# A copy kernel with staged batches: six buffers for four, loads and stores in long runs, remainders eight batches late

## The chip, the cores and the metric

The kernel runs on one core of a Trainium2 chip. The metric is the device time of one execution in microseconds (us); lower is better. A *span* is the length of one profiled execution; it is about 1.8 us shorter than the time of the same run. For the kernel before, its span of 757.3 us would go with some 759 us (an estimate from that 1.8), 2 us above its median: the first profile before is one of its slower executions.

## The reference, cut to what matters

```python
batch, length, dim = (32, 4096, 256)          # float32
window_size, stride = 64, 32
n_windows = (length - window_size) // stride + 1      # 127
for i in range(n_windows):
    start = i * stride
    result[:, i] = x[:, start:start + window_size].copy()
```

It is pure copying. A batch of x is 128 blocks of 32 rows, 32 KB each; a window is two neighbouring blocks, 64 KB. So almost every block is written twice.

## The kernel before: the parts that matter

There are two ways for a batch, on two queues.

- **Direct** (21 batches, issued from the Sync engine, q1 in the profile): DRAM to DRAM copies of 16 windows at a time, seven of them a batch. Some are split in two copies, of the first and the second halves of the windows. Fifteen windows remain: the *remainder*.
- **Staged** (11 batches, issued from the Scalar engine, q10 in the profile): the batch is loaded once into a buffer of 128 partitions and stored twice, once for the first halves of the windows, once for the second halves.

A staged store writes 128 half windows where only 127 are its own. The odd one spills into the neighbouring batch, so a remainder of that neighbour may be written only after the stores have landed. That is why the remainders are late, and why they wait.

```python
class Staging:
    ...
    def load(self, q, g):
        n, i = divmod(g, len(self.tiles))
        if n:
            q.wait_ge(self.stored[i], 32 * n)
        self.c.load(q, self.tiles[i], self.batches[g]).then_inc(self.loaded[i], 16)

    def store(self, q, g):
        n, i = divmod(g, len(self.tiles))
        q.wait_ge(self.loaded[i], 16 * (n + 1))
        ...  # the last batch: four smaller stores
        for half in (0, 1):
            self.c.store(q, self.tiles[i], self.batches[g], half).then_inc(self.stored[i], 16)

    def run(self, q):
        bufs = len(self.tiles)
        for g in range(min(bufs, len(self.batches))):
            self.load(q, g)
        for g in range(len(self.batches)):
            self.store(q, g)

            if g >= 1 and g - 1 + bufs < len(self.batches):
                self.load(q, g - 1 + bufs)
...
    staged = [*range(1, B - 3, 3), B - 2]
    st = Staging(c, pool, x.dtype, staged, 4)
    ring_d, ring_s = nc.sync, nc.scalar
    ...
    def rest(b):                    # the remainder of direct batch b, 15 windows
        for n in (b - 1, b + 1):
            if n in spilled:
                st.wait_stored(ring_d, spilled.index(n))
        c.windows(ring_d, b, 0 if b - 1 in spilled else 112, 15)
    ...
        late = 4
        for i, b in enumerate(direct):
            w0 = 15 if b - 1 in spilled else 0
            for j in range(7):
                ...  # 16 windows, in one copy or in two
            if b in free:
                rest(b)
            elif i >= len(free) + late:
                rest(direct[i - late])
        for b in direct[-late:]:
            rest(b)
        ring_d.wait_ge(c.done, c.total)
```

Of the kernel before, what the change touches and what calls it, by code (L numbers as in the profile page):

```python
# [1 line left out]

# [4 lines left out]


DIRECT, IN, OUT = 32768, 16384, 16384


class Copier:


    def __init__(self, nc, tc, x, out, B, L, D, W, S, n_win):
        assert W == 2 * S and L % S == 0
        self.nc, self.tc, self.x, self.out = nc, tc, x, out
        self.B = B
        self.blk = S * D
        self.nb = L // S  # L20
        self.nw = n_win
        self.total = 0
        self.done = tc.alloc_semaphore("done")

    def xap(self, block, dims):
        return bass.AP(self.x.tensor, self.x.offset + block * self.blk, dims)

    def oap(self, elem, dims):
        return bass.AP(self.out.tensor, self.out.offset + elem, dims)

    def count(self, dma):
        dma.then_inc(self.done, 16)
        self.total += 16

    def windows(self, q, b, w0, n, half=None):

        blk = self.blk
        size = 2 * blk if half is None else blk
        off = blk if half else 0
        self.count(  # L40
            q.dma_start(
                out=self.oap((b * self.nw + w0) * 2 * blk + off, [[2 * blk, n], [1, size]]),
                in_=bass.AP(
                    self.x.tensor,
                    self.x.offset + (b * self.nb + w0) * blk + off,
                    [[blk, n], [1, size]],
                ),
                max_dma_last_dim=DIRECT,
            )
        )  # L50

    def load(self, q, t, b):
        return q.dma_start(
            out=t[:, :], in_=self.xap(b * self.nb, [[self.blk, self.nb], [1, self.blk]]),
            max_dma_last_dim=IN,
        )

    def store(self, q, t, b, half, p0=0, n=None):



        blk = self.blk
        n = self.nb if n is None else n
        w = b * self.nw + p0 - half
        return q.dma_start(
            out=self.oap(w * 2 * blk + half * blk, [[2 * blk, n], [1, blk]]),
            in_=t[p0 : p0 + n, :],
            max_dma_last_dim=OUT,
        )


class Staging:


    def __init__(self, c, pool, dtype, batches, bufs):
        self.c, self.batches = c, batches
        self.tiles = [pool.tile([128, c.blk], dtype, name=f"xb{i}") for i in range(bufs)]
        self.loaded = [c.tc.alloc_semaphore(f"loaded{i}") for i in range(bufs)]
        self.stored = [c.tc.alloc_semaphore(f"stored{i}") for i in range(bufs)]
# [10 lines that stand above are left out]
        if g == len(self.batches) - 1:  # L90

            for half, p0, rows in ((0, 0, 112), (0, 112, 15), (1, 1, 15), (1, 16, 112)):
                self.c.count(self.c.store(q, self.tiles[i], self.batches[g], half, p0, rows))
            return
        for half in (0, 1):
            self.c.store(q, self.tiles[i], self.batches[g], half).then_inc(self.stored[i], 16)

    def wait_stored(self, q, g):
        n, i = divmod(g, len(self.tiles))
        q.wait_ge(self.stored[i], 32 * (n + 1))  # L100

    def run(self, q):
        bufs = len(self.tiles)
        for g in range(min(bufs, len(self.batches))):
            self.load(q, g)
        for g in range(len(self.batches)):
            self.store(q, g)

            if g >= 1 and g - 1 + bufs < len(self.batches):
                self.load(q, g - 1 + bufs)  # L110


@with_exitstack
def kernel(
    ctx: ExitStack,
    tc: tile.TileContext,
    x: bass.AP,
    window_size: bass.AP,
    stride: bass.AP,
    out: bass.AP,  # L120
):
    nc = tc.nc
    W, S = int(window_size), int(stride)
    B, L, D = x.shape
    n_win = (L - W) // S + 1
    assert out.shape == (B, n_win, W, D)
    c = Copier(nc, tc, x, out, B, L, D, W, S, n_win)
    staged = [*range(1, B - 3, 3), B - 2]
    direct = [b for b in range(B) if b not in staged]
    pool = ctx.enter_context(tc.tile_pool(name="xb", bufs=1))  # L130
    st = Staging(c, pool, x.dtype, staged, 4)
    ring_d, ring_s = nc.sync, nc.scalar
    spilled = staged[:-1]

    def rest(b):
# [6 lines that stand above are left out]
    with tc.tile_critical():  # L142
        st.run(ring_s)



        free = [b for b in direct if b - 1 not in spilled and b + 1 not in spilled]
        direct = free + [b for b in direct if b not in free]
        late = 4
        for i, b in enumerate(direct):  # L150
            w0 = 15 if b - 1 in spilled else 0
            for j in range(7):
                if j % 3 == 1 or (j == 3 and i % 5 != 2):
                    c.windows(ring_d, b, w0 + 16 * j, 16, 0)
                    c.windows(ring_d, b, w0 + 16 * j, 16, 1)
                else:
                    c.windows(ring_d, b, w0 + 16 * j, 16)
# [9 lines that stand above are left out]
# [1 line left out]
_INS = ['x', 'window_size', 'stride']  # L168
_OUTS = [((32, 127, 64, 256), 'float32')]

_NUMBERS = {'window_size': 64, 'stride': 32}


# [26 lines left out]
```

## Time and profile before

| | before |
|---|---|
| time, median | 756.73 us (756.65 to 757.59, 4 runs) |
| moved by the DMA engines | 313.16 MB |
| share of 16 DMA engines, q1 and q10 | 55.2% and 44.1% |
| waits of the Sync queue on staged stores | 100.2 us in 6 waits |

The page of the profile: the busy tenths of the DMA engines and their GB/s in 40 slices of the span, then the two queues with packets, MB and the time of their packets as a share of 16 engines' span.

```profile
DMA  9999999999999999999999999999999999999996
GB/s 372 429 400 423 409 431 426 420 420 408 408 435 418 408 413 430 408 413 434 431 403 418 425 411 408 425 426 402 416 422 428 393 428 423 419 425 422 415 398 294
...
q1 hardware_dynamic: 8945, 174.80, 55.2%
q10 hardware_dynamic: 9002, 138.35, 44.1%
```

The DMA engines are busy from start to end; nothing else works. But "busy" is not "as fast as they can": the rate goes up and down between about 400 and 435 GB/s, and dips come back every three or four slices. That beat was in view before the prediction, and it turned out to be what the case is about: the seven moments at which q10 goes from stores to a load lie in slices 10, 14, 17, 21, 24, 28 and 32 (found from the packet records, below), and these slices show 408, 408, 408, 403, 411, 402 and 393 GB/s.

The view of stretches, at the end of the kernel before (start and end in us, length, other engines, clock, share of the DMA engines, GB/s):

```profile
700.00:720.00 20.00, 0.00 (x0) 1.00 0.99 416
720.00:740.00 20.00, 0.00 (x0) 1.00 0.94 397
740.00:757.00 17.00, 0.00 (x0) 1.00 0.68 292
```

A share of 0.94 is 15 engines of 16: the remainders have 15 rows, and one engine gets nothing of them and ends early.

The waits of the Sync queue (line and what it waited for; us in all, times, longest), and the DMA issues of the staged batches (out, in, count, size, median us from issue to landing):

```profile
SPq L41 <- DMA out_dram<-xb: 100.2, 6, 42.7
SPq L142 <- DMA out_dram<-in_x_dram: 47.8, 1, 47.8
...
out_dram<-xb ACTq DMA_DIRECT2D x20, 4096.0 KB, 115.1
xb<-in_x_dram ACTq DMA_DIRECT2D x11, 4096.0 KB, 90.0
```

A wait of 42.7 us need not cost anything: a copy lands about 95 us after its issue, so there is work queued for longer than the wait.

### The profile page before, as it was taken

How to read it: one execution, taken by the hardware profiler on the slowest of the kernel's cores; microseconds unless marked ns; L12 is line 12 of the kernel's file. 1: busy time of each engine (PE TensorE's matmuls, PEld its weight loads, DVE VectorE, ACT ScalarE, POOL GpSimd, SP SyncE). 2: the span in 40 equal slices, each digit the busy share in tenths (PEclk: the TensorE clock that was granted, in tenths of full speed). 3: DMA queues.
4: the chain of work that ended last, by engine and by line, in shares of the span. 5: the costliest groups of instructions: out<-in, count | busy, mean ns of one | idle time of the engine just before them, and what ended most of it. 6: DMA issues, size and time to landing. Idle time of an engine off the chain costs nothing. (4 is left out here: it accounts for less than half of the span.)

```text
span 757.3 us, 312 instructions
## 1 busy us (share of the span) xinstructions
POOL 0.2 (0%) x4
## 2 busy tenths in 40 slices
POOL 0000000000000000000000000000000000000000
DMA  9999999999999999999999999999999999999996
GB/s 372 429 400 423 409 431 426 420 420 408 408 435 418 408 413 430 408 413 434 431 403 418 425 411 408 425 426 402 416 422 428 393 428 423 419 425 422 415 398 294
DMA packets 17949, 313.16 MB, mean 414 GB/s; under 512 B 4169, under 2 KB 4169, under 8 KB 4169
## 3 DMA queue, kind: packets, MB, share of 16 engines
q1 hardware_dynamic: 8945, 174.80, 55.2%
q10 hardware_dynamic: 9002, 138.35, 44.1%
q14 instruction: 2, 0.02, 0.0%
HBM read 220.92 MB, written 266.99 MB: 644 GB/s over the span
## 5 line engine op out<-in xcount | busy, mean ns | idle before, releaser
L181 POOL MEMSET const-bfloat16-1.0<- 128x1 bf16 x1 | 0.1, 102 | 0.0
L181 POOL MEMSET const-uint8-127<- 128x1 uint8 x1 | 0.1, 102 | 0.0
L181 POOL MEMSET const-float32-0.0<- 128x1 f32 x1 | 0.1, 99 | 0.2 <-issue 0.2
L181 POOL MEMSET const-float32-1.0<- 128x1 f32 x1 | 0.1, 99 | 0.0
## 6 DMA issues: line engine op xcount, KB each, us to landing
out_dram<-in_x_dram SPq DMA_DIRECT2D x88, 1024.0 KB, 95.2
out_dram<-xb ACTq DMA_DIRECT2D x20, 4096.0 KB, 115.1
out_dram<-in_x_dram SPq DMA_DIRECT2D x118, 512.0 KB, 94.4
xb<-in_x_dram ACTq DMA_DIRECT2D x11, 4096.0 KB, 90.0
out_dram<-in_x_dram SPq DMA_DIRECT2D x21, 960.0 KB, 95.0
out_dram<-xb ACTq DMA_DIRECT2D x2, 3584.0 KB, 93.4
out_dram<-xb ACTq DMA_DIRECT2D x2, 480.0 KB, 94.9
```

What stands on the lines that cost most here:

```text
L181: nc = _bacc.Bacc("TRN2", target_bir_lowering=False, num_devices=1)
```

## The change

Three things at once: six buffers of 4 MB in place of four; on the Scalar queue six loads in a row, then their twelve stores, then the other five loads and their stores; and the remainders of the direct batches eight batches late and not four.

```diff
     def run(self, q):
         bufs = len(self.tiles)
-        for g in range(min(bufs, len(self.batches))):
-            self.load(q, g)
-        for g in range(len(self.batches)):
-            self.store(q, g)
-
-            if g >= 1 and g - 1 + bufs < len(self.batches):
-                self.load(q, g - 1 + bufs)
+        for first in range(0, len(self.batches), bufs):
+            group = range(first, min(first + bufs, len(self.batches)))
+            for g in group:
+                self.load(q, g)
+            for g in group:
+                self.store(q, g)
...
-    st = Staging(c, pool, x.dtype, staged, 4)
+    st = Staging(c, pool, x.dtype, staged, 6)
...
-        late = 4
+        late = 8
```

Number, size and bytes of all copies stay the same.

## The prediction

> **What bounds the kernel now.** The DMA engines. The page's row of slices shows them 90% or more busy in 39 of 40 slices; the queue table gives q1 (direct DRAM to DRAM copies) 55.2% and q10 (staged loads and stores) 44.1% of 16 engines' span: 99.3% together, 313.16 MB in 757.3 us. Bytes over engine time is 26 GB/s an engine for either queue. The Trainium skill says why (DMA: Bandwidth & Descriptors, "Issuing engines are not separate DMA queues": all queues run on the same 16 engines and interleave); this trace agrees.
>
> The last stretch: the view of stretches gives an engine share of 0.99 for 700 to 720 us, 0.94 for 720 to 740, 0.68 after. 0.94 is 15/16. The remainders have 15 rows; by the same page's section on the increment by 16 such a copy runs on 15 engines. So one engine has about 1.4 MB less than the others (22 MB of 15-row copies / 15) and ends some 40 us early, in any order of issue. The other 15 end within about 5 us of one another, and q10 about 5 us before q1. Little idle time is left to win.
>
> **What the change removes, adds, moves.** Same DMAs, sizes, and bytes on each engine. Only order and waits change.
> - Scalar queue: instead of one load, two stores in turn, 6 loads, 12 stores, 5 loads, the last 12 stores. In the trace, total throughput while q10 loads is about 415 GB/s, while it stores 420 to 430; in the first run of four loads (411 to 419) as in the single loads later (409 to 418). The amounts are unchanged, so longer runs move about 0: estimate -2 to +3 us. Second-round loads wait for stores issued long before; q10 should keep at least four 4 MB copies outstanding.
> - Sync queue: the waits view gives 100.2 us in 6 waits on staged stores (longest 42.7) and 47.8 at the very end. They cost nothing now: issue to landing is 95 us, about 29 copies stand outstanding, and q1 does not dip in those waits. Eight late removes the early ones (estimate: 40 us, mainly one of 33 near 105 us), worth 0.
> - The end: 8 remainders instead of 4 are issued last. The last staged batch but one still has 8.1 MB of stores behind it on q10, so its last store lands near 703 us (now 706), and only its two remainders (1.9 MB, about 5 us) wait for it, with some 9 MB of q1 still queued. The other six find their stores done or wait behind a full queue. 0 to +3 us.
>
> **On the critical path:** almost nothing of it. The chain is the 15 fuller engines' own bytes, 19.7 MB each at about 26.3 GB/s, 748 us, plus 2 us of start and some 5 of uneven end.
>
> **Prediction:** 757 us, 8 times in 10 between 751 and 762. Faster by over 2%: 0.02; within 2%: 0.95; slower by over 2%: 0.03.
>
> **What would show it:** engine share 0.99 to about 715 us, queue bytes unchanged, mean near 414 GB/s, 405 to 420 in the load runs and 415 to 432 in the store runs; Sync waits of about 90 us, all late, without a dip.
>
> **What would make it wrong:** long runs having another rate than short ones; one queue ending well before the other; second-round loads stalling on stores (a drop of q10); late remainders finding q1 empty (share well under 0.9 before 740 us).

## More of the kernel before

The experiments came in three sets, each on one chip with its own runs of the kernel before. The level differs a little between them (the kernel before took 756.7 us in the first comparison, with the changed kernel, and 751.0, 749.2 and 751.2 us in the three sets), so times are compared within a set, by ratios.

By the packet records 15 engines are busy from about 717 to 747 us.

In the old order q10 goes from stores to a load seven times; in the new order once.

## The result, and the profile after

A ratio in this text is the one of one kernel's runs to those of the kernel before in the same comparison; it is not quite the ratio of the medians quoted.

| | before | after |
|---|---|---|
| median | 756.73 us | 752.93 us |
| runs | 756.65 to 757.59 (4) | 752.16 to 756.21 (4) |
| ratio, 95% interval | | 0.9958 (0.9935 to 0.9980) |
| span of the profiled run | 757.3 us | 751.0 us |

The changed kernel is 0.4% faster: within 2% as forecast, inside the range, and a small gain that the interval keeps clear of nothing. In set 2 (below) it was 0.6%. The page of the changed kernel:

```profile
DMA  9999999999999999999999999999999999999996
GB/s 373 418 413 428 407 419 424 428 427 428 428 427 427 426 430 422 428 417 428 421 428 403 413 423 421 421 425 418 423 427 418 428 414 427 414 433 420 416 398 293
...
q1 hardware_dynamic: 8945, 174.80, 55.1%
q10 hardware_dynamic: 9002, 138.35, 44.2%
```

Same bytes, same shares, same first and last slices. What is gone is the beat: slices 8 to 19 now hold between 417 and 430, where before they swung between 408 and 435. The one change that is left comes at 403 us, in slice 22, and that slice shows 403 GB/s. Its end, its waits and its issues:

```profile
700.00:720.00 20.00, 0.00 (x0) 1.00 0.96 406
720.00:740.00 20.00, 0.00 (x0) 1.00 0.94 401
740.00:751.00 11.00, 0.00 (x0) 1.00 0.51 219
```

```profile
SPq L41 <- DMA out_dram<-xb: 56.0, 2, 41.5
SPq L141 <- DMA out_dram<-in_x_dram: 49.4, 1, 49.4
...
out_dram<-xb ACTq DMA_DIRECT2D x20, 4096.0 KB, 138.5
xb<-in_x_dram ACTq DMA_DIRECT2D x11, 4096.0 KB, 133.6
```

The end is the same with 15 engines (by the packet records from about 709 to 741 us), only some 6 us sooner. The waits on staged stores fell from 100.2 to 56.0 us. The staged copies stand longer in their queue (134 to 139 us to landing for 90 to 115): the queue is deeper. So there were three candidates for the gain.

**Where the time went, from the packet records.** The trace lists every DMA packet with its duration. The usual one is 1213 ns for a packet of 32 KB on q1 and 611 ns for one of 16 KB on q10 (the medians, in both kernels). Call what a packet takes over that its *excess*, and sum it over all packets, divided by 16 engines. That gives 22.9 us before and 16.4 us after: 6.5 us less, where the span is 6.3 us shorter. (The medians differ by 3.8 us only, since the profile before is of a slower execution.) The gain is thus packets that ran at their usual speed instead of longer, not idle time that was filled.

Where the long packets stand is not random. Counting those that start from 3 us before to 10 us after q10 goes from stores to a load (the moment at which 2% of the load's packets have started; up to 690 us of the span), the kernel before has 7.6 us of excess at its seven changes and the changed kernel 0.7 us at its one. The packets of both queues are long there: of the 7.6 us, 4.1 are on q1 and 3.6 on q10. At the changes back, from load to stores (3 us either side), it is 1.5 us at eight and 0.6 us at two. Some of what is gained there comes back during the rest of the loads (5.3 us before, 7.0 after).

The view of stretches says the same more coarsely: two of the seven single loads of the kernel before, then the second run of five loads of the changed kernel.

```profile
180.00:203.00 23.00, 0.00 (x0) 1.00 1.00 407
248.00:271.00 23.00, 0.00 (x0) 1.00 1.01 407
...
404.00:514.00 110.00, 0.00 (x0) 1.00 1.01 420
```

All seven single loads move 403 to 416 GB/s in total, 411 in the mean, over 154 us of stretches. At 420 these would take some 3 us less (an estimate from these views), which is about half of the 6.3 us between the spans (the stretches leave out the first us around each change). The store runs move 422 to 426 before and 423 to 425 after.

### The profile page after: what moved, and what is told of

Same layout as the page of the kernel before. It is cut to its first block, busy times and chain, and to the rows that moved or that the text cites. A ratio compares the mean times of both kernels' runs of the same rounds, so it can differ in the third digit from the quotient of the medians.

```text
span 751.0 us, 312 instructions
## 1 busy us (share of the span) xinstructions
POOL 0.2 (0%) x4
```

## The experiments

The theories, one for each part of the change:

- **G, or S in the later sets (switches):** what costs is that q10 goes from stores to a load; long runs of loads and of stores avoid it.
- **D (depth):** six buffers let a load be issued long after the stores it waits for, and keep more staged copies outstanding.
- **R (remainders):** the 15-row remainders disturb the direct copies, and pay when they come later.

### Each part alone

Set 1, 5 rounds; the kernel before took 750.97 us here (749.41 to 752.25, 11 runs).

`late8_only`, the remainders alone:

```diff
-        late = 4
+        late = 8
```

> Four buffers and the old order of loads and stores; only the remainders are 8 late. Theory R (remainders: the gain of 0.42% comes from the 15-row remainders starting later): ratio to before about 0.996, 753 us. Theory G (long runs of loads and of stores are what is cheaper): 1.000, 756.7 us. Theory D (depth: six buffers keep more staged copies outstanding): 1.000.

Measured: 750.64 us, ratio 0.9994 (0.9981 to 1.0006). The waits on staged stores are those of the full change, 56.0 us where the profile of the kernel before has 100.2:

```profile
SPq L41 <- DMA out_dram<-xb: 56.0, 2, 41.8
```

So R falls, and those 44 us of waits were worth nothing, as the prediction had said of them.

`groups6_late4`, the changed kernel with the remainders as before:

```diff
-        late = 8
+        late = 4
```

> Six buffers, runs of six loads and twelve stores, remainders 4 late as before. Theory R: ratio 1.000, 756.7 us. Theory G: 0.996, 753 us. Theory D: 0.996.

Measured: 745.29 us, ratio 0.9923 (0.9909 to 0.9936). The whole gain is there without the later remainders. Its waits on staged stores are 228.1 us in 8 waits, more than twice those of the kernel before, and it is faster all the same: once more the waits cost nothing.

`six_old_order`, six buffers in the kernel before and nothing else (its rule then makes six loads first, and one load and two stores in turn after that, with five changes from stores to a load):

```diff
-    st = Staging(c, pool, x.dtype, staged, 4)
+    st = Staging(c, pool, x.dtype, staged, 6)
```

> Six buffers, but the old order after the first loads (one load, two stores in turn), remainders 4 late. Theory R: 1.000. Theory G: about 1.000 (only the first run is longer), 756.7 us. Theory D: 0.996, 753 us.

Measured: 748.70 us, ratio 0.9968 (0.9955 to 0.9981). This is less than half of what groups6_late4 gained with the same buffers. It is a larger gain than the 1.000 that was written for G, and D's 0.996 lies within the interval: this run alone does not part the two. But the longer first run also takes two changes away, which the expectation for G had passed over.

`groups4_late4`, the runs with four buffers (4, 4 and 3 batches; two changes from stores to a load):

```diff
-    st = Staging(c, pool, x.dtype, staged, 6)
+    st = Staging(c, pool, x.dtype, staged, 4)
...
-        late = 8
+        late = 4
```

> Four buffers, runs of four loads and eight stores (4, 4 and 3 batches), remainders 4 late. Theory R: 1.000. Theory G: 0.997 to 0.998, 754 to 755 us, part of the gain. Theory D: 1.000.

Measured: 747.04 us, ratio 0.9948 (0.9934 to 0.9961). More than half of the gain needs no more buffers, only the order; it is more than the 0.997 to 0.998 that was written for G. D alone can't give that.

### Depth against order, and the remainders once more

Set 2, 5 rounds; the kernel before took 749.22 us (749.03 to 751.52, 11 runs).

`after_again` is the changed kernel, and `groups6_late4_b` is groups6_late4 a second time, to have both on one chip.

> The changed kernel once more, to be compared on one chip with the same kernel at 4 late. If the remainders' place is worth nothing: ratio to before as groups6_late4_b within 0.002 (0.992 to 0.994). If eight late costs: 0.995 to 0.996 as on the first chip, against 0.992.

> As groups6_late4 in the earlier runs, of which this is the same kernel: ratio to before 0.992 (0.990 to 0.994).

Measured: 744.72 us, ratio 0.9938 (0.9922 to 0.9955), for after_again; 745.22 us, 0.9939 (0.9926 to 0.9952), for groups6_late4_b. Four or eight batches late makes no difference that these rounds can show.

`six_same_order` has six buffers and yet exactly the old order of instructions on the Scalar queue:

```diff
-    st = Staging(c, pool, x.dtype, staged, 4)
+    st = Staging(c, pool, x.dtype, staged, 6)
...
     def run(self, q):
-        bufs = len(self.tiles)
+        bufs = 4
```

> Exactly the old order of instructions on the Scalar queue, with its seven changes from stores to a load, but six buffers, so that a load waits for stores issued long before; late 4. Theory S (each change of q10 from stores to loads costs about 1 us of longer packets): ratio 1.000. Theory D (what was dear is a load that waits for stores just issued, q10 running short): 0.994 or below.

Measured: 749.80 us, ratio 0.9998 (0.9984 to 1.0012). The staged copies stand about as long in their queue as in the changed kernel (136 to 138 us to landing, for 134 to 139), so the queue is about as deep. Two more buffers and a deeper queue are worth nothing while the order stays. D falls; buffers count only as far as they allow longer runs.

The two traces of this set show the cause beside each other. The view of stretches of six_same_order, for a piece of its steady part: stretches of 43 us (two stores) and of 20 to 22 us (one load) in turn.

```profile
201.00:244.00 43.00, 0.00 (x0) 1.00 1.00 426
245.00:267.00 22.00, 0.00 (x0) 1.00 0.99 411
269.00:312.00 43.00, 0.00 (x0) 1.00 1.00 426
313.00:334.00 21.00, 0.00 (x0) 1.00 1.00 414
336.00:379.00 43.00, 0.00 (x0) 1.00 1.01 429
381.00:401.00 20.00, 0.00 (x0) 1.00 1.01 415
```

And of after_again: its twelve stores, its second run of five loads, the last stores but the very end.

```profile
134.00:397.00 263.00, 0.00 (x0) 1.00 1.01 429
399.00:509.00 110.00, 0.00 (x0) 1.00 1.01 427
511.00:685.00 174.00, 0.00 (x0) 1.00 1.01 429
```

Engines are equally busy in all of these. A single load between stores runs at 411 to 415 GB/s in total (407 to 417 over all seven), five loads in a row at 427, nearly as fast as stores. Cut in eight equal parts, the seven single loads of six_same_order have mean packet times on q10 of 642, 763, 658, 630, 614, 614, 617 and 658 ns: the long packets stand at the beginning, and some at the end where stores follow. The five loads of after_again that have three or more loads ahead of them in their run have 620, 626, 626, 626, 641, 628, 614 and 635 ns: the hump is gone.

### More changes instead of fewer

`half_loads` (set 2) was to double the dose. On six_same_order, each load is two loads of 64 rows; for the seven later ones, one half goes between the two stores of a batch and one after them. That makes 14 changes.

```diff
...  (load takes one half of the rows; store calls its third argument between its two stores)
-            self.load(q, g)
-        for g in range(len(self.batches)):
-            self.store(q, g)
-
-            if g >= 1 and g - 1 + bufs < len(self.batches):
-                self.load(q, g - 1 + bufs)
+            self.load(q, g, 0)
+            self.load(q, g, 1)
+        for g in range(len(self.batches)):
+            nxt = g - 1 + bufs
+            more = g >= 1 and nxt < len(self.batches)
+            self.store(q, g, (lambda: self.load(q, nxt, 0)) if more else (lambda: None))
+            if more:
+                self.load(q, nxt, 1)
```

> As six_same_order, but every load is two loads of 64 rows, and of the seven later ones one half goes between the two stores and one after them: same bytes, 14 changes from stores to loads instead of 7. Theory S: 6 to 8 us slower than six_same_order, ratio about 1.008 to 1.010. Theory D or any that counts bytes or waits: 1.000, as six_same_order.

Measured: 767.0 us, ratio 1.0227 (1.0209 to 1.0246). It is slower, but by more than twice what S had said, and its trace shows that part of it lies in the first 60 us, where no change occurs at all. So it needed a control.

`half_loads_together` (set 3) has the same halves, one right after the other, with seven changes:

```diff
-            self.store(q, g, (lambda: self.load(q, nxt, 0)) if more else (lambda: None))
+            self.store(q, g)
             if more:
+                self.load(q, nxt, 0)
                 self.load(q, nxt, 1)
```

> The control for half_loads: six buffers, every load in two copies of 64 rows, but both halves one after the other, so seven changes of q10 from stores to loads and not 14. half_loads lost 17 us, of which its trace shows about 8 in the first 55 us, where the order is the same as here. Theory S: about 1.010 to 1.013 to before (757 to 759 where before is 749), the first 55 us slow as in half_loads; half_loads is 6 to 9 us above it. Rival: 64-row loads are dear wherever they stand and the changes cost nothing: 1.022 as half_loads.

Measured: 771.5 us (765.82 to 776.79), ratio 1.0286 (1.0243 to 1.0328), where the kernel before took 751.23 us in set 3. The control is not faster than half_loads; it is rather slower. By the total the rival holds for this pair: loads of 64 rows are dear, and the forecast of S, half_loads 6 to 9 us above its control, failed. The start of half_loads_together, and then a stretch in its first stores, from the view of stretches:

```profile
2.00:20.00 18.00, 0.00 (x0) 1.00 1.00 306
20.00:40.00 20.00, 0.00 (x0) 1.00 1.00 326
40.00:60.00 20.00, 0.00 (x0) 1.00 1.01 373
106.00:126.00 20.00, 0.00 (x0) 1.00 1.00 432
```

six_same_order, with loads of 128 rows, runs at 421, 423 and 428 GB/s in the first three of these stretches. The lesson is of method too: the dose was doubled by a means that had a price of its own.

But the traces show that this price is not paid everywhere, and where it is not, S is seen. The surplus of half_loads_together over half_loads stands at the start (60 MB are moved by 156.6 us, against 151.9) and at the very end (the last 23 MB take 66.4 us, against 61.7). The changes lie between. The view of stretches from 170 to 620 us, of six_same_order (7 changes), half_loads_together (7) and half_loads (13 of its 14), in this order:

```profile
170.00:620.00 450.00, 0.00 (x0) 1.00 1.01 422
170.00:620.00 450.00, 0.00 (x0) 1.00 1.01 421
170.00:620.00 450.00, 0.00 (x0) 1.00 1.00 417
```

From the packet records, the time from 60 MB moved to 290 MB moved is 543.0, 544.7 and 549.6 us: halving the loads costs 1.7 us here, and seven more changes 4.9, about 0.7 us each. The excess at the changes, counted as above, is 7.1, 5.6 and 12.4 us. So in this part half_loads does speak for S, in dose too. This was read from single traces after the totals were known, and half_loads_together ran on another chip than the other two.

`two_ahead` (set 3) adds changes with loads of full size: two loads first and then two stores and one load in turn, which makes nine changes. Six buffers, so that no load waits for anything recent.

```diff
-        bufs = 4
+        bufs = 2
...
-            if g >= 1 and g - 1 + bufs < len(self.batches):
-                self.load(q, g - 1 + bufs)
+            if g + bufs < len(self.batches):
+                self.load(q, g + bufs)
```

(The lines are those of six_same_order.)

> Six buffers, loads of full size, but only two loads first and then two stores and one load in turn: nine changes from stores to loads instead of seven, no load waits for anything recent, late 4. Theory S at about 1 us a change: 1.002 to 1.003, 751 us where before is 749. Rival, that only depth or buffers count: 1.000 or below.

Measured: 752.47 us, ratio 1.0027 (1.0009 to 1.0045). Slower, as S had it. The step is small, but its interval leaves out 1. (The profiled run is the slowest of its six, 755.15 us, so its span in the table below is on the high side.)

With loads of full size, then, changes from stores to a load and time go together over the whole row:

| kernel | changes | ratio to before | excess of the packets, us | of it at the changes | span, us |
|---|---|---|---|---|---|
| two_ahead | 9 | 1.0027 | 16.5 | 6.4 | 753.4 |
| six_same_order | 7 | 0.9998 | 14.0 | 7.1 | 748.8 |
| late8_only | 7 | 0.9994 | 13.9 | 5.1 | 749.5 |
| six_old_order | 5 | 0.9968 | 12.9 | 3.8 | 747.0 |
| groups4_late4 | 2 | 0.9948 | 10.3 | 1.4 | 744.2 |
| groups6_late4 | 1 | 0.9923 | 8.4 | 0.8 | 744.5 |
| groups6_late4_b | 1 | 0.9939 | 8.2 | 0.7 | 743.1 |
| after_again | 1 | 0.9938 | 7.8 | 0.6 | 742.5 |

From nine changes to one (the mean of the last three, 0.9933) the ratio falls by 0.0094, which is about 0.9 us a change at 750 us. The packets that stand at the changes give 0.6 to 1.0 us for each, in every one of these traces. Span less excess is 733.9 to 736.9 us in all eight, and 734.4 and 734.6 us in the first two profiles: most of what these kernels differ by is packets that take longer than usual.

Two rivals lie in the same row. The number of loads at the very start differs too (2, 4 or 6), but kernels with the same start differ as their changes do: with four, late8_only and groups4_late4 (7 and 2 changes, 0.9994 and 0.9948); with six, six_old_order and groups6_late4 (5 and 1, 0.9968 and 0.9923). And each kernel has just one change back, from loads to stores, more than changes to a load, so the row can't tell which of the two directions costs. Only the place of the long packets does: 7.1 us at the seven changes to a load and 2.0 at the eight changes back in six_same_order, 6.4 at nine and 3.3 at ten in two_ahead. Most of the cost, not all, stands at the change to a load.

### Two tries at more

`groups6_late20` (set 3): all 20 dependent remainders at the very end.

```diff
-        late = 8
+        late = 20
```

> Six buffers in runs of six, and all 20 dependent remainders at the very end. If their place is worth nothing, as 4 and 8 late were alike on one chip: 0.993 to 0.995. If late remainders find q1 short of work or crowd 15 engines at the end: above 0.996, and an engine share under 0.93 before the last 15 us.

Measured: 743.36 us, ratio 0.9900 (0.9884 to 0.9917). It is the fastest kernel of this study, and better than what was expected of either side. Its excess is 6.3 us, its span 741.0 us. The late remainders do not starve q1: the waits on staged stores are 57.4 us in all, and the share of the engines stays at 0.94 to the last 20 us, the figure of 15 engines.

```profile
700.00:720.00 20.00, 0.00 (x0) 1.00 0.94 397
720.00:741.00 21.00, 0.00 (x0) 1.00 0.71 304
```

Whether 20 late is better than 4 or 8 is not settled: those ran in other sets, on other chips (0.9923 to 0.9939), the intervals of groups6_late20 and groups6_late4 overlap, and the difference of 0.002 to 0.004 is not much larger than what the changed kernel showed between two comparisons (0.9958 and 0.9938).

`rest16` (set 3): groups6_late4 with each remainder cut in 16 column pieces of 4 KB, so that it runs on 16 engines.

```diff
+    def spread(self, q, b, w0, n):
+        blk, cut = self.blk, self.blk // 8
+        self.count(
+            q.dma_start(
+                out=self.oap((b * self.nw + w0) * 2 * blk, [[cut, 16], [2 * blk, n], [1, cut]]),
+                in_=self.xap(b * self.nb + w0, [[cut, 16], [blk, n], [1, cut]]),
+                max_dma_last_dim=DIRECT,
+            )
+        )
...
-        c.windows(ring_d, b, 0 if b - 1 in spilled else 112, 15)
+        c.spread(ring_d, b, 0 if b - 1 in spilled else 112, 15)
```

> groups6_late4 with the 15-row remainders cut into 16 column pieces of 4 KB, so that they run on 16 engines and the sixteenth no longer ends early. If pieces of 4 KB move as fast as those of 32 KB: 3 us less than groups6_late4, ratio 0.989 to 0.991, and no stretch of 0.94 share before the end. If small pieces cost more than the balance gives: 0.994 or above.

Measured: 772.76 us, ratio 1.0296 (1.0267 to 1.0325): a loss of 3%. But not because small pieces move slowly: while such pieces are in flight beside q10 the total is as high as ever. The view of stretches, two in the middle and two near the end:

```profile
440.00:460.00 20.00, 0.00 (x0) 1.00 1.00 427
500.00:520.00 20.00, 0.00 (x0) 1.00 1.03 439
640.00:660.00 20.00, 0.00 (x0) 1.00 1.01 324
700.00:720.00 20.00, 0.00 (x0) 1.00 1.02 343
```

From the packet records: between 500 and 520 us q10 moves 261 GB/s and q1 170, 431 together, where it is 190 and 240 in the first store run of after_again, with the old remainders. (The view of stretches counts a packet where it starts, hence 439; the records here spread it over its time.) Small packets on q1 and a larger share for q10 go together over the whole run: cut from 60 to 620 us in stretches of 10 us, q10 moves 302 GB/s in the 12 stretches with more than 40 GB/s of small packets and 193 in the 36 with under 5. So q10 was through at 629 us, and q1 went on alone for 140 us, most of them at 324 to 343 GB/s, with the engines busy: its packets of 32 KB took 1526 ns there (the median from 640 to 740 us) and not 1213. The balance came as hoped: 16 engines are busy to about 760 us, where groups6_late4 has 15 from about 702 to 734 us, and the idle time of an engine in the mean fell from 6.9 to 3.9 us. But the two queues no longer end together. More staged batches might mend that; it was not tried.

## Why the prediction was right, and where not

- **The range held:** 757 us with 751 to 762, measured 752.93. That is partly luck: 757 us was no gain at all, and the gain of 3.8 us fell outside the sum's own terms (-2 to +3 us for the queue, 0 to +3 for the end) but inside a wider range. The bound was named rightly: DMA engines, same bytes, nearly no idle time.
- **The waits were worth nothing, as said.** late8_only took 44 us of Sync waits away for a ratio of 0.9994. The size in the prediction's list ("about 90 us") did not follow from its own subtraction (148 us less 40 is 108); measured were 56.0 us on staged stores and 49.4 at the end, 105.4 in all.
- **The end was as said:** one engine ends early in any order (0.94 in both kernels), and eight or even twenty late remainders do not find q1 empty. The second round of loads did not leave q10 short: it takes 134 us from issue to landing of a load, so as much work stands queued.
- **The term that was mis-sized:** "The amounts are unchanged, so longer runs move about 0: estimate -2 to +3 us." The measured gain was 3.8 us between the medians, 4.5 us in set 2. The step under it was that loads run at about 415 GB/s "in the first run of four loads (411 to 419) as in the single loads later (409 to 418)". Two ranges of slices that overlap were taken as equal. Measured over the loads themselves, the single ones move 411 GB/s in the mean and the second run of loads of the changed kernel 420; in set 2 it is 407 to 417 against 427. (That the first run is no fair sample, because it holds the start of the kernel, is likely but not shown.) Both figures lie in the "405 to 420 in the load runs" that the prediction gave as its sign, so that sign could not have told the two cases apart. The prediction's own list had "long runs having another rate than short ones" as its first way to be wrong, and that is what occurred, by half a per cent.
- **What was in view and not used:** the beat of dips in the row of slices. Averages by kind (load, store) hid that the long packets stand around the changes between the kinds. Sorting packets by distance from a change would have shown 7.6 us of excess at seven changes.
- **What stays open:** why a change costs. A change, and a first load after stores, are the same event in these kernels, and no run parts them. The pair with loads of 64 rows, meant to strengthen S, does so only in the middle of its traces; why such loads are slow in the first 60 us is open. And in the first comparison the stores had about 7 us of excess away from changes in both kernels (1.4 us in six_same_order and 2.8 in after_again, of set 2); nothing explains that.

## What to carry to other kernels

When the DMA engines are busy all the time and bytes are fixed, look at how long packets take beside their usual time, and where the long ones stand; idle time and waits say nothing then. In this kernel a queue that goes from stores to a load pays about 0.9 us each time, so buffers are best spent on long runs of one kind, and buffers without the longer runs gave nothing. Change the order before the buffers, and check that two queues still end together when the size of copies on one of them changes.

## What the Trainium skill lacked or had wrong

- **DMA: Bandwidth & Descriptors, the rules on queues and bandwidth:** nothing on the order of loads and stores within a queue. The runs show about 0.9 us for each change from stores to a load of 4 MB (1.0027 of the time at nine changes, 0.993 at one), with engines busy all along.
- **The same page, "Issuing engines are not separate DMA queues",** says that several issuing engines save only the time to initiate copies. The totals agree while both queues have work (431 GB/s with 170 on q1 and 261 on q10, in rest16, and 429 in the first store run of after_again with 240 and 190). They do not once one queue is empty: q1 by itself, with DRAM to DRAM copies alone, moved 324 to 343 GB/s in rest16. Whether that is from the one queue or from the kind of copy, no run tells.
- **The same page, "Queues, rings and completion order",** says that an engine takes turns between queues by packets. No run shows the turns as such, but the shares go the way that this suggests. What happens to them when one queue's pieces are small is not said: with 4 KB pieces among those of 32 KB on q1, q10 rose from about 190 to 261 GB/s and the balance of the two queues was lost, for 3% of the time.
- **The same page, rules for kernel authors,** advises against two transfers to disjoint halves of the partitions because they gain nothing. The runs show that they can cost: with loads of 64 rows in place of 128 the ratio went from 1.000 to 1.029 with the order kept (half_loads_together), and the first 60 us ran at 306 to 373 GB/s. Later in the kernel it was little: 1.7 us from 60 to 290 MB.
- **The same page, on why a DMA increments its semaphore by 16 (how many engines a copy uses):** agrees. Copies of 15 rows left one engine idle, seen as a share of 0.94 near the end of the kernel before, of the changed one and of groups6_late20; in rest16, where they run on 16, all 16 are busy to about 760 us.
